# One wait for all casts of a group, in place of a wait per quarter, ahead of TensorE's transposes

## The chip, the cores and the metric

The kernel runs on one core of a Trainium2 chip. The metric is device microseconds of one execution, taken as the median of several.

## The reference

```python
def setup_inputs():
    b1, b2, m, k, n = 8, 16, 256, 512, 384
    return {"x": randn(b1, b2, m, k), "weight": randn(b1, b2, k, n)}   # float32 (cut)

def reference(x, weight):
    return np.matmul(x, weight).astype(np.float32)
```

These are 128 independent products of 256x512 by 512x384.

## The kernel before

Four products make a group, and there are 32 groups. SyncE issues all transfers: for each group two loads of w, one of x, and one store. ScalarE casts x to bfloat16 in four quarters (q). TensorE transposes each quarter (two bfloat16 values packed in a float32 word), VectorE copies the transposed quarter out of PSUM, TensorE multiplies, ScalarE copies the product to `out_sb`. VectorE also casts w.

```python
    XS, WS, OS = 2, 2 * G // D, 4       # buffers of x (groups), w (halves), out (groups)
    BS, TS, WBS = 1, 2, 2 * G           # of cast x, transposed x, cast w
    PT, PO = 4, 2                       # PSUM tiles: transposes, products
    LAG = 4                             # loads run four groups ahead of the stores
    ...
    def load(e, t, U, s):               # SyncE: two w loads, then the x load
        ...
                e.wait_ge(w_cast, n * (G * S) + ((d + 1) * D * S - 2 * G * S))
        ...
            e.wait_ge(x_cast, n * T + (1 - XS) * T)
    ...
    def multiply(e, t, U, s):           # TensorE
        n = t * U + s
        words = x_bf[s % BS][:].rearrange("p r s q c -> p r (s q c)").bitcast(fp32)
        for q in range(T):
            e.wait_ge(x_cast, n * T + (q + 1))
            e.wait_ge(t_copied, n * T + (q + 1 - PT + BIAS))
            for rr in range(2):
                for h in range(KO // 2):
                    ins = e.transpose(
                        pt[(s * T + q) % PT][:, rr, h, :],
                        words[:, 2 * q + rr, h :: KO // 2],
                        identity[:],
                    )
            ins.then_inc(t_made, 1)
        e.wait_ge(w_cast, n * (G * S) + G * S)
        for q in range(T):
            e.wait_ge(t_copied, n * T + (q + 1 + BIAS))
            e.wait_ge(o_copied, n * T + (q + 1 - PO + BIAS))
            for rr in range(2):
                for ko in range(KO):
                    for i in range(G):              # four products side by side
                        mine = slice(i * C, (i + 1) * C)
                        ins = e.matmul(po[...][mine, rr, :N], x_t[...], w_bf[...], ...)
            ins.then_inc(p_made, 1)
    ...
    def on_sync(e):
        ...
                load(e, t, U, LAG + s)
                store(e, t, U, s)
```

The order in the one transfer queue is thus w, w, x of group n+4, then the store of group n: a store always goes out behind an x.

## Time and profile before

| | before |
|---|---|
| median of 3 runs, us | 518.9 (518.43 to 518.95) |
| span of the profiled run, us | 517.2 |
| DMA queue, share of 16 engines' time | 99.3% |
| busiest compute engine (VectorE) | 64% |
| TensorE matmul / weight load | 59% / 39% |

The table is read from the bottom up: no compute engine is near the span, and the transfers fill it. The prediction below shows the lines. In the timeline, ScalarE's casts are followed in brackets by ScalarE's idle time before them and by what ended it. That idle time is the room between the chain of compute and the arrival of x:

```profile
114.30 3.89 ACT L132 CAST x_bf<-x_sb 128x1024 bf16<-128x1024 f32 x4 [3.76 <-DMA x_sb<-in_x_dram]
...
241.52 3.89 ACT L132 CAST x_bf<-x_sb 128x1024 bf16<-128x1024 f32 x4 [4.21 <-DMA x_sb<-in_x_dram]
```

### The profile page before, as it was taken

To read this page: it belongs to the slowest core of one execution; us is meant where nothing else is said; L and a number is where in the kernel's file an instruction comes from. 1 tells how busy PE (TensorE), PEld (TensorE's weight loads), DVE (VectorE), ACT (ScalarE), POOL (GpSimd) and SP (SyncE) were. 2 spreads that over 40 slices of the span, in tenths; PEclk is the share of its full clock that TensorE was granted. 3 is DMA by queue.
4 is the path that set the end of the run, shared out by engine and by line. 5 is a ranking of instruction groups with operands and counts; after the bars stand their busy time and mean duration, and the time that the engine had idled before them with its cause. 6 is when DMAs were issued, how large, how long until landed. Compare 5 with 4: busy or idle time off the path is not lost.

```text
span 517.2 us, 11523 instructions
## 1 busy us (share of the span) xinstructions
PE 306.6 (59%) x4608; PEld 200.6 (39%) x4608; DVE 332.8 (64%) x384; ACT 236.7 (46%) x264; POOL 0.7 (0%) x6
## 2 busy tenths in 40 slices
PE   0478776556665457645577554776446765467752
PEld 0345444334443334433344332444324443244431
DVE  3698875667556676556675566855658656676550
ACT  0465564443644436435355354454444544544441
POOL 0000000000000000000000000000000000000000
PEclk9998877878777887878777778877788877778777
DMA  8999999999999999999999999999999999999996
GB/s 340 430 423 424 424 432 426 429 428 430 432 427 427 427 428 432 429 427 430 426 431 431 426 429 430 427 432 427 427 429 429 427 433 425 430 428 430 429 428 251
DMA packets 18869, 218.18 MB, mean 422 GB/s; under 512 B 2096, under 2 KB 2096, under 8 KB 2608
## 3 DMA queue, kind: packets, MB, share of 16 engines
q1 hardware_dynamic: 18864, 218.11, 99.3%
q8 instruction: 3, 0.05, 0.0%
q14 instruction: 2, 0.02, 0.0%
HBM read 167.77 MB, written 50.33 MB: 422 GB/s over the span
## 4 chain that ended last, share of the span: by engine, by line
DMA 81%; ACT 10%; PE 4%; issue 3%; ACTq 0%; SPq 0%
DMA x_sb<-in_x_dram 81%; ACT x_bf L132 9%; PE po L180 2%; PE pt L166 1%; ACTq L130 0%; ACT out_sb L194 0%; SPq L111 0%; SPq L103 0%; ACT L132 0%; ACTq L193 0%; SPq L282 0%; SPq L55 0%
## 5 line engine op out<-in xcount | busy, mean ns | idle before, releaser
L147 DVE CAST w_bf<-w_sb 64x1536 bf16<-64x1536 f32 x256 | 244.4, 955 | 47.2 <-DMA w_sb<-in_weight_dram 38.5
L166 PE MATMUL pt<-identity,x_bf 128*128 128x128 f32 x512 | 123.7, 425 | 199.3 <-ACT x_bf L132 199.1
L180 PE MATMUL po<-w_bf,x_t 128*32 128x384 bf16 x4096 | 185.1, 342 | 1.0 <-issue 1.0
L166 PEld LDWEIGHTS pt<-identity,x_bf 128*128 128x128 f32 x512 | 91.8, 216 | 232.1 <-issue 218.3
L194 ACT COPY out_sb<-po 128x768 f32<-128x768 f32 x128 | 102.2, 798 | 147.2 <-PE po L180 147.2
L153 DVE COPY x_t<-pt 128x1024 bf16<-128x1024 bf16 x128 | 88.4, 691 | 122.3 <-PE pt L166 121.8
L132 ACT CAST x_bf<-x_sb 128x1024 bf16<-128x1024 f32 x128 | 124.4, 1042 | 80.9 <-DMA x_sb<-in_x_dram 80.8
L180 PEld LDWEIGHTS po<-w_bf,x_t 128*32 128x32 bf16 x4096 | 108.8, 101 | 73.8 <-issue 14.2
L132 ACT ACT_TABLE_LOAD x8 | 10.3, 1283 | 42.9 <-DMA x_sb<-in_x_dram 42.9
masks.py:199 POOL TENSOR_SCALAR_AFFINE_SELECT identity<-identity 128x128 f32<-128x128 f32 x1 | 0.3, 292 | 0.2 <-POOL identity L200 0.2
L200 POOL MEMSET identity<- 128x128 f32 x1 | 0.2, 204 | 0.5 <-SPq L55 0.5
L271 POOL MEMSET const-bfloat16-1.0<- 128x1 bf16 x1 | 0.1, 101 | 0.0
L271 POOL MEMSET const-uint8-127<- 128x1 uint8 x1 | 0.1, 101 | 0.0
L271 POOL MEMSET const-float32-0.0<- 128x1 f32 x1 | 0.1, 98 | 0.2 <-issue 0.2
L271 POOL MEMSET const-float32-1.0<- 128x1 f32 x1 | 0.1, 98 | 0.0
## 6 DMA issues: line engine op xcount, KB each, us to landing
w_sb<-in_weight_dram SPq DMA_DIRECT2D x64, 1536.0 KB, 27.5
x_sb<-in_x_dram SPq DMA_DIRECT2D x32, 2048.0 KB, 27.5
out_dram<-out_sb SPq DMA_DIRECT2D x31, 1536.0 KB, 30.7
out_dram<-out_sb SPq DMA_DIRECT2D x4, 384.0 KB, 5.9
```

The costliest lines, as they stand in the source:

```text
L132: e.copy(out=x_bf[s % BS][:, rows], in_=x_sb[s % XS][:, rows].rearrange("p r (q s c) -> p r s q c", s=S, c=KO),).then_inc(x_cast, 1)
L147: e.tensor_copy(out=w_bf[(s * G + d * D + a) % WBS][h * HP : (h + 1) * HP], in_=w_sb[slot][a * HP : (a + 1) * HP, h * KO : (h + 1) * KO, : ...
L153: e.tensor_copy(out=x_t[s % TS][:, 2 * q : 2 * q + 2], in_=pt[(s * T + q) % PT][:].bitcast(bf16),).then_inc(t_copied, 1)
L166: ins = e.transpose(pt[(s * T + q) % PT][:, rr, h, :], words[:, 2 * q + rr, h :: KO // 2], identity[:],)
L180: ins = e.matmul(po[(s * T + q) % PO][mine, rr, :N], x_t[s % TS][:, 2 * q + rr, ko // 2, mine, ko % 2], w_bf[(s * G + i) % WBS][:, ko, :], ...
L194: e.copy(out=out_sb[s % OS][:, 2 * q : 2 * q + 2, :], in_=po[(s * T + q) % PO][:, :, :N],).then_inc(o_copied, 1)
L200: e.memset(identity[:], 0.0).then_inc(id_done, 1)
L271: nc = _bacc.Bacc("TRN2", target_bir_lowering=False, num_devices=1)
```

## The change

TensorE waits until all four quarters of a group's x are cast, then does its 16 transposes in one run. The intent: TensorE rests while the casts run, which is when the store queued behind that x goes out.

```diff
         words = x_bf[s % BS][:].rearrange("p r s q c -> p r (s q c)").bitcast(fp32)
+
+        e.wait_ge(x_cast, n * T + T)
         for q in range(T):
-            e.wait_ge(x_cast, n * T + (q + 1))
             e.wait_ge(t_copied, n * T + (q + 1 - PT + BIAS))
```

## The prediction

> **What bounds the kernel now.** I read the page first: how busy the engines are against the DMA, and what share of the DMA queue's time is used.
>
> ```profile
> PE 306.6 (59%) x4608; PEld 200.6 (39%) x4608; DVE 332.8 (64%) x384; ACT 236.7 (46%) x264; POOL 0.7 (0%) x6
> ...
> DMA  8999999999999999999999999999999999999996
> ...
> q1 hardware_dynamic: 18864, 218.11, 99.3%
> ...
> HBM read 167.77 MB, written 50.33 MB: 422 GB/s over the span
> ...
> DMA 81%; ACT 10%; PE 4%; issue 3%; ACTq 0%; SPq 0%
> ```
>
> No compute engine is busy for more than 64% of the 517.2 us span, while the 16 DMA engines are busy for 99.3% of it and show a 9 in all slices but the first and last. The chain that ended last is 81% loading of x. Each group moves 2 x 1536 KB of w, 2048 KB of x and 1536 KB of out, 6.82 MB. Over 32 groups that is 218 MB, which at 429 GB/s takes 508 us. What is left is the start and the end. So the question for the change is not how long TensorE takes, but whether the DMA queue ever runs empty because of it.
>
> Next I asked for engine times in chosen stretches (columns: stretch, its length, busy us and count of PE, PEld, DVE, ACT, POOL, then TensorE clock, DMA share, GB/s).
>
> ```profile
> 4.00:16.00 12.00, 0.00 (x0) 0.00 (x0) 7.07 (x8) 0.00 (x0) 0.00 (x0) 1.00 1.01 431
> 100.00:300.00 200.00, 124.75 (x1860) 81.67 (x1862) 130.97 (x152) 93.26 (x105) 0.00 (x0) 0.78 1.01 429
> 498.00:501.00 3.00, 3.00 (x14) 2.34 (x15) 1.50 (x3) 2.55 (x3) 0.00 (x0) 0.50 1.01 430
> 502.00:506.00 4.00, 4.00 (x104) 2.71 (x100) 0.29 (x1) 1.97 (x3) 0.00 (x0) 1.00 1.00 424
> 514.00:516.00 2.00, 0.00 (x0) 0.00 (x0) 0.00 (x0) 0.00 (x0) 0.00 (x0) 0.50 0.04 17
> ```
>
> The reader is to see that the DMA moves 431 GB/s with TensorE wholly idle, 429 in the steady state, and 430 in a stretch where TensorE does nothing but transposes. The rate does not follow TensorE.
>
> Third, one group in the order of time, which gives the length of every step that the change touches.
>
> ```profile
> 258.69 3.89 ACT L132 CAST x_bf<-x_sb 128x1024 bf16<-128x1024 f32 x4
> 259.86 0.73 PEld L166 LDWEIGHTS pt<-identity,x_bf 128*128 128x128 f32 x4 [7.32 <-issue]
> 259.87 3.96 PE L166 MATMUL pt<-identity,x_bf 128*128 128x128 f32 x16 [6.94 <-ACT x_bf L132]
> 260.80 0.73 PEld L166 LDWEIGHTS pt<-identity,x_bf 128*128 128x128 f32 x4 [0.21 <-issue]
> ...
> 262.75 0.33 SPq L111 DMA_DIRECT2D x_sb<-in_x_dram  x1
> ...
> 273.31 3.89 ACT L132 CAST x_bf<-x_sb 128x1024 bf16<-128x1024 f32 x4 [2.41 <-DMA x_sb<-in_x_dram]
> ```
>
> Four casts take 3.89 us. TensorE follows them one by one: 0.73 us of transposes, a gap of about 0.22, the next four. The load of the x two groups later is issued 0.17 us after the last cast (258.69 + 3.89 = 262.58), and does not wait for TensorE.
>
> **What the Trainium skill says.** (1) "DMA: Bandwidth & Descriptors", Specifications, gives a fabric ceiling of 435 GB/s for a core's 16 DMA engines. The trace agrees: 429 to 431 GB/s, so at most 1.4% could be won from a better rate. (2) "SBUF — State Buffer", Who interferes with whom: DMA never contends with a compute engine. The trace agrees, 431 against 429 to 430 as shown. So letting TensorE rest while a store goes out has no transfer to speed up. (3) "TensorE: Matmul & The Clock Gate", Part 1: the clock is half until the engine has been busy for a window of 3413 ns. The trace shows a clock of 0.50 in 498 to 501 us, at the start of a run, and 1.00 in 502 to 506, so a shorter run of transposes may leave more matmuls at the half clock.
>
> **The change, part by part.** It removes three of four waits on the casts per group and makes the first wait for all four. It moves the 16 transposes; it adds and removes no work of an engine.
>
> (a) Start of the transposes: now after the first cast (1.04 us), then after the fourth (3.89), so 2.85 us later.
> (b) Their length: now the cast pace, 3 x 0.95 + 0.73 = 3.6 us. Then 4 x 0.73 = 2.9 us without gaps (an estimate from the 0.73; VectorE's copies of 0.69 us keep up with this, and the four PSUM buffers that they need were emptied in the group before).
> (c) So the matmuls start 2.85 + 2.9 - 3.6 = 2.1 us later. Clock: if the transposes' run is 0.7 us shorter, some 0.7 us more of the matmuls falls at half clock, which costs about 0.35 us on average. Sum: each group's copy to out_sb ends 2.1 to 2.6 us later, and so do VectorE's copies and the next w casts behind them.
>
> None of this is on the path that sets the end while the DMA queue has work. An x load takes a median of 27.5 us from issue to landing, of which its own 2.1 MB at 429 GB/s is 4.9 us. The other 22 us are other transfers ahead of it: that is the slack. A w load (27.5 us, 3.7 of its own) has 24 us. Against that, w loads come 2.1 to 2.6 us later and x loads not at all, unless ScalarE is late. Its idle time before the casts in the steady state is 2.41 to 4.79 us, so at worst a cast starts 0.2 us late.
>
> **The start** is tighter. There ScalarE is idle for under 1 us before the casts of groups 2 to 4 (0.28, 0.95, 0.24), so the delay adds up: about 2.2 us for each of the first five or six groups, some 8 to 10 us at most. Then it shrinks, because a group's chain on ScalarE (casts to last copy: 12 us now, 14.4 then, and 1.3 more in one of four) is still shorter than the 15.9 us that the DMA needs for a group. In those groups an x load lands 20 to 24 us after issue, so 15 to 19 us of slack, which covers it. Counting bytes issued against 429 GB/s, I find at least some 7 us of queued work at each issue (estimate).
>
> **The end** is where a delay could show in full. From the timeline, and the landing times of the stores issued at 492.9 us (group 30) and at 507.7 us (the last quarter of group 31):
>
> ```profile
> 501.49 5.38 PE L180 MATMUL po<-w_bf,x_t 128*32 128x384 bf16 x128
> ...
> 506.92 0.80 ACT L194 COPY out_sb<-po 128x768 f32<-128x768 f32 x1 [0.50 <-PE po L180]
> ```
>
> ```profile
> DMA to landing us min/median/max: 19.2/19.2/19.2
> ```
>
> ```profile
> DMA to landing us min/median/max: 8.0/8.0/8.0
> ```
>
> Group 30's store lands at 492.9 + 19.2 = 512.1. The four quarters behind it, 1.57 MB, take 3.7 us at 429 GB/s, and the last lands at 507.7 + 8.0 = 515.7, just 3.6 us after. So the slowest DMA engine was working off stores back to back up to the end (the others ran dry about 512: share 0.22, then 0.04), and the last piece sat in its queue. How late may that piece come? The first w load took 7.7 us from an empty queue, 3.7 of it transfer, so 4.0 us of latency; a quarter needs 4.0 + 0.9 = 4.9. Issued 2.1 to 2.6 us later, at 509.8 to 510.3, it would land at 514.7 to 515.2, still before 515.7. I expect 0 here, 0.5 us at the outside. **Sum**: 0 in the middle, 0 at the start, 0 to 0.5 at the end.
>
> **The rivals.**
> - The delay reaches the end: the engines that ran dry at 512 us show that the queue is nearly empty there. If the slowest engine is less slow in the next run, all 2.1 to 2.6 us show: 521.0 to 521.5, slower by 0.5%. Against it: 515.7 - 512.1 is the bare transfer time.
> - The store is helped by a resting TensorE, as the change intends. All stores are 50.3 MB, some 117 us at 429 GB/s. If these alone ran at 435, 1.6 us would be won, and at that rate throughout 7 us (512). Against it: 431 GB/s with TensorE idle, and the store is issued after the casts and lands 30.7 us later (page, section 6), so what goes out just then is older work anyway.
> - ScalarE or VectorE becomes the bound through the longer chain: about 14.4 us a group plus 1.3/4 is under 15.9, with 1 us to spare. If the matmuls fell to half clock altogether (LDWEIGHTS of four per 0.32 us instead of 0.16, so up to 10 us instead of 5.4), the chain would be 18 us and the kernel 8 to 13% slower. For it: TensorE idles longer before a run. Against it: the clock needs one busy window, and transposes plus matmuls are a run of over 8 us.
>
> **The range and the chances.** Now 518.9, with three runs from 518.43 to 518.95. My sum adds 0 to 0.5; I say 519.0. The low edge, 518.1, is a run as good as the best with a little of the second rival; the high edge, 520.4, is most of the first rival. 2% is 10 us: slower needs a bound that changes (the third rival, 1%), faster needs more than the whole gap to the fabric ceiling (1%). Within 2%: 98%.
>
> **What would show it right or wrong.** In the profile after: DMA still at 9 throughout and about 429 GB/s; TensorE's wait for the casts moved to one wait per group; 16 transposes in some 2.9 us; the matmuls some 2.1 us later after the casts' start (now 263.75 - 258.69 = 5.1, then about 7.2); ScalarE's idle time before the casts shorter by 2 us; x loads landing after nearly the same 27.5 us; the last store piece issued some 2 us later and landing in less than 8.0 us. I am wrong if slices in the middle show a DMA share below 9, if the x casts start later than x lands in the steady state, or if the rate differs from 429 by over 1%.

## The result

| | before | after |
|---|---|---|
| median of 6 runs, us | 518.64 (518.33 to 518.95) | 519.20 (518.98 to 519.51) |
| ratio, 95% interval | | 1.0011 (0.9998 to 1.0024) |
| span of the profiled run, us | 517.2 | 517.7 |

A ratio here is the mean time of one kernel's fast runs over that of the other's fast runs of the same rounds, so it is not quite the ratio of the medians. The two are the same within 2%. The difference of 0.56 us is small against the interval, but no run of after was as fast as the slowest of before, so I looked for it as well.

The page of after, the lines that answer to those of before:

```profile
PE 300.4 (58%) x4608; PEld 212.9 (41%) x4608; DVE 332.9 (64%) x384; ACT 235.9 (46%) x264; POOL 0.7 (0%) x6
...
DMA  8999999999999999999999999999999999999995
...
q1 hardware_dynamic: 18864, 218.11, 99.2%
...
DMA 56%; PE 22%; ACT 15%; issue 5%; ACTq 1%; SPq 0%
```

The DMA is as full as before. The chain that ended last, though, has lost a third of its x loads to TensorE and ScalarE: for part of the run, the chain of compute no longer waits for x. The time hardly moved, which is a warning that a chain's shares are not a cost.

One group of after in the steady state, from the timeline:

```profile
259.43 3.88 ACT L132 CAST x_bf<-x_sb 128x1024 bf16<-128x1024 f32 x4
263.44 3.29 PEld L167 LDWEIGHTS pt<-identity,x_bf 128*128 128x128 f32 x16 [8.17 <-issue]
263.45 3.68 PE L167 MATMUL pt<-identity,x_bf 128*128 128x128 f32 x16 [7.79 <-ACT x_bf L132]
263.49 0.33 SPq L111 DMA_DIRECT2D x_sb<-in_x_dram  x1
...
267.06 5.74 PE L181 MATMUL po<-w_bf,x_t 128*32 128x384 bf16 x128
...
274.08 3.88 ACT L132 CAST x_bf<-x_sb 128x1024 bf16<-128x1024 f32 x4 [0.42 <-DMA x_sb<-in_x_dram]
```

The matmuls of the matching group of before (its casts, at 258.69, stand in the prediction):

```profile
263.75 6.29 PE L180 MATMUL po<-w_bf,x_t 128*32 128x384 bf16 x128
```

The transposes are one run now, and the matmuls start 7.63 us after the casts' start (267.06 - 259.43), where before it was 5.06 (263.75 - 258.69): 2.57 us later. The load of the next x is still issued just after the last cast. ScalarE's room before the casts went from 2.41 to 0.42 us in the matching group.

In the first third of the run that room is gone altogether. These casts follow ScalarE's own earlier work without a wait, until the last line, the first with a wait for x since the first group:

```profile
106.19 3.88 ACT L132 CAST x_bf<-x_sb 128x1024 bf16<-128x1024 f32 x4
119.94 3.88 ACT L132 CAST x_bf<-x_sb 128x1024 bf16<-128x1024 f32 x4
...
178.51 3.88 ACT L132 CAST x_bf<-x_sb 128x1024 bf16<-128x1024 f32 x4 [0.46 <-DMA x_sb<-in_x_dram]
```

And the end. The last piece of the store is issued at 512.0 us in after (507.7 before) and lands in 4.3 us instead of 8.0, so at 516.3 instead of 515.7.

```profile
501.17 3.68 PE L167 MATMUL pt<-identity,x_bf 128*128 128x128 f32 x16 [6.54 <-ACT x_bf L132]
...
504.78 6.33 PE L181 MATMUL po<-w_bf,x_t 128*32 128x384 bf16 x128
...
511.17 0.80 ACT L195 COPY out_sb<-po 128x768 f32<-128x768 f32 x1 [0.50 <-PE po L181]
```

So the last group's compute ended 4.25 us later (511.17 against 506.92), and the program ended 0.5 us later.

### The profile page after: what moved, and what is told of

It reads as the page before. It is cut to its first block, busy times and chain, and to the rows that moved or that the text cites. A ratio compares the mean times of both kernels' runs of the same rounds, so it can differ in the third digit from the quotient of the medians.

```text
span 517.7 us, 11427 instructions
## 1 busy us (share of the span) xinstructions
PE 300.4 (58%) x4608; PEld 212.9 (41%) x4608; DVE 332.9 (64%) x384; ACT 235.9 (46%) x264; POOL 0.7 (0%) x6
## 3 DMA queue, kind: packets, MB, share of 16 engines
q1 hardware_dynamic: 18864, 218.11, 99.2%
## 4 chain that ended last, share of the span: by engine, by line
DMA 56%; PE 22%; ACT 15%; issue 5%; ACTq 1%; SPq 0%
DMA x_sb<-in_x_dram 56%; PE po L181 14%; ACT x_bf L132 14%; PE pt L167 8%; ACT L132 1%; ACTq L130 1%; ACT out_sb L195 0%; SPq L103 0%; SPq L111 0%; ACTq L194 0%; ACTq L246 0%; SPq L283 0%; SPq L55 0%
## 5 line engine op out<-in xcount | busy, mean ns | idle before, releaser
L167 PE MATMUL pt<-identity,x_bf 128*128 128x128 f32 x512 | 115.8, 418 | 210.8 <-ACT x_bf L132 210.8
L167 PEld LDWEIGHTS pt<-identity,x_bf 128*128 128x128 f32 x512 | 104.0, 225 | 222.6 <-issue 222.6
L181 PEld LDWEIGHTS po<-w_bf,x_t 128*32 128x32 bf16 x4096 | 109.0, 102 | 75.2 <-issue 16.1
## 6 DMA issues: line engine op xcount, KB each, us to landing
w_sb<-in_weight_dram SPq DMA_DIRECT2D x64, 1536.0 KB, 25.2
x_sb<-in_x_dram SPq DMA_DIRECT2D x32, 2048.0 KB, 26.4
```

The source lines that it names most:

```text
L167: ins = e.transpose(pt[(s * T + q) % PT][:, rr, h, :], words[:, 2 * q + rr, h :: KO // 2], identity[:],)
L181: ins = e.matmul(po[(s * T + q) % PO][mine, rr, :N], x_t[s % TS][:, 2 * q + rr, ko // 2, mine, ko % 2], w_bf[(s * G + i) % WBS][:, ko, :], ...
```

## The experiments

**Theory 1**: the transfers set the end; the queue hides the delay, and the end hides nearly all of it. **Rival, steady state**: the small loss comes from the groups in the middle, from a transfer rate that depends on what TensorE does. **Rival, any delay shows**. Twelve kernels ran, in three calls; each call had its own runs of before, on its own chip.

### Where is the 0.5 us?

First the changed kernel once more, as a yardstick.

> The changed kernel unaltered, as a yardstick beside the others of this call. Both theories: about 0.5 us above before (0.1%), as in the first result (519.2 against 518.64), if that difference is real; if it is run-to-run noise, anything from -0.3 to +0.6 us.

Measured: 519.06 us against 518.66 of before, ratio 1.0012 (0.9998 to 1.0026). So the 0.4 to 0.56 us came twice, though this time the fastest run of after (518.85) was not slower than the slowest of before (518.92).

Next, the new wait in all groups but the last (`late` is the changed wait):

```diff
-        with nc.Fori(0, NG // U, ...) as t:
+        with nc.Fori(0, NG // U - 1, ...) as t:
             for s in range(U):
-                multiply(e, t, U, s)
+                multiply(e, t, U, s, late=True)
+        multiply(e, 0, NG, NG - 2, late=True)
+        multiply(e, 0, NG, NG - 1, late=False)
```

> The late transposes in the first 31 groups, the old interleaving in the last one. Theory 1 (the queue hides the delay in the steady state, and what little shows comes from the end): as before, 518.6, within 0.2 us. Rival (the small loss comes from the steady state, from a transfer rate that depends on what TensorE does): about 519.2, as the changed kernel.

Measured: 519.39 us, ratio 1.0013 (0.9999 to 1.0026). And the reverse, with `late` true in the last group alone:

> The old interleaving in the first 31 groups, the late transposes in the last one alone. Theory 1: between 518.6 and 519.2; all of the small loss if the end carries it, with the last store piece issued some 2.5 to 4 us later than in before and landing in about 4 to 5 us instead of 8. Rival (steady state): 518.6, as before.

Measured: 518.68 us, ratio 1.0000 (0.9986 to 1.0014).

This went against theory 1 in its second half. The end costs nothing that shows: with the delay in the last group only, the last piece is issued at 510.3 us and lands 5.2 us later, at 515.5. With the last group early it is issued at 508.6 and lands 7.6 us later, at 516.2. The small loss goes with the first 31 groups. That rests on the medians and on the runs (all 519.16 or more, against 518.92 at most for before); the intervals of the ratios overlap.

### Does the transfer rate depend on TensorE?

All compute removed; a load waits for the landing of the load that had its buffer (out is zero):

```diff
-                e.wait_ge(w_cast, ...)            # and x_cast for x, o_copied for stores
+                e.wait_ge(w_in[slot], ...)        # and x_in for x; stores: the memsets alone
-    on_gpsimd; on_vector; on_tensor; on_scalar
+    for o in out_sb: nc.vector.memset(o[:], 0.0)
```

> The same loads and stores in the same order, with no cast, transpose, matmul or copy (out is zero: wrong on purpose). A load waits for the landing of the load that had its buffer, so two groups are in flight. It shows what the transfers alone cost when TensorE rests all the time. Theory 1: 516 to 519 us, i.e. at most 0.5% under before, at the same 429 GB/s in the middle. Rival (TensorE's work slows the stores, and rest helps them): 1 to 2% under before, 508 to 513 us, with a rate in the middle of 433 GB/s or more.

Measured: 517.32 us, ratio 0.9977 (0.9964 to 0.9991). The whole of the compute, with TensorE's work in it, costs this kernel 0.23%. That is the most that any rest of TensorE could win.

The opposite: before, with 16 dummy transposes after each group's matmuls.

```diff
             ins.then_inc(p_made, 1)
+        for _ in range(16):
+            e.transpose(pt[(s * T) % PT][:, 0, 0, :], identity[:], identity[:])
```

> The kernel before with 16 dummy transposes after each group's matmuls, in TensorE's idle time (the gap there is 4.4 us or more in the steady state; they take some 3.3 us), so that TensorE rests far less while stores go out. Theory 1: 518.6 as before, within 0.3 us, 429 GB/s in the middle. Rival (TensorE's activity slows the transfers): slower by 0.3% or more, and a lower rate.

Measured: 518.94 us against 518.86, ratio 1.0001 (0.9987 to 1.0015), TensorE busy 70% instead of 59%. Nothing. But these are transposes; matmuls beside a store are tested further down.

### How much delay is hidden?

The changed kernel with 4, 8 and 16 dummy transposes ahead of each group's first one:

```diff
+            if q == 0:
+                for _ in range(extra):            # 4, 8 or 16
+                    e.transpose(pt[(s * T) % PT][:, 0, 0, :], identity[:], identity[:])
```

> The changed kernel with 4 more transposes (of the identity, into a buffer that is overwritten) ahead of each group's 16, some 0.8 us more delay a group. In the fill of the changed kernel one group's chain on ScalarE takes 14.4 us on average; this makes 15.3, still under the DMA's 15.9. Theory 1: within 1 us of the changed kernel, 519 to 520.5. Rival (any delay shows): 519.2 + 32 x 0.8 = 545.

> 8 more transposes a group, some 1.65 us. The chain takes 16.1 us, just over the DMA's 15.9: theory 1 has the kernel bound by the chain now, 32 x 16.1 + 17.4 to the first x, less what the last group does not need, some 523 to 535 us, and the DMA share falling below 9 tenths or ScalarE no longer waiting for x. Rival (the transfers bound it whatever TensorE does): 519 to 520.

> 16 more transposes a group, some 3.3 us. Chain 17.7 us. Theory 1: 17.4 + 32 x 17.7 + about 5 = 585 to 595 us, slower by 13%, which shows where the slack ends. Rival (hidden whatever it is): 519 to 523.

| extra transposes a group | time, us | ratio to before | DMA rate |
|---|---|---|---|
| 0 (the change, first result) | 519.20 | 1.0011 | 429 (100 to 300 us) |
| 4 | 519.73 | 1.0018 | 429 (60 to 460 us) |
| 8 | 521.37 | 1.0049 | 429 (60 to 460 us) |
| 16 | 542.36 | 1.0466 | 421 (60 to 460 us) |

The rates come from the stretches of the two traces (columns as in the prediction), with 8 and with 16:

```profile
60.00:460.00 400.00, 262.00 (x3900) 204.16 (x3893) 264.50 (x308) 191.24 (x215) 0.00 (x0) 0.83 1.01 429
```

```profile
60.00:460.00 400.00, 273.11 (x3977) 219.72 (x3976) 253.40 (x300) 182.16 (x206) 0.00 (x0) 0.82 1.01 421
```

The slack does end, at the place where the chain of a group passes the 15.9 us that its transfers need. With 16 the chain took 16.2 us (four groups from 180.63 to 245.49), and 32 of these plus the 17.4 us to the first x is 536, with the last store still to come. I had expected 17.7 a group and 585 to 595 us; with 8 a group took 15.4 (217.54 to 278.98), not 16.1, and the 521.37 us lie between the two ranges (519 to 520 and 523 to 535), so both missed. The reason is in the timeline: the extra transposes bring TensorE to its full clock sooner, so that the 16 real ones run faster. With 16 extra ones:

```profile
204.31 2.08 PE L172 MATMUL pt<-identity,x_bf 128*128 128x128 f32 x16
206.32 5.38 PE L186 MATMUL po<-w_bf,x_t 128*32 128x384 bf16 x128
```

The clock is 1.00 from 204.3 us on here, and 0.50 in the run of transposes shown for after (263.4 to 267.06). The 16 real transposes take 2.08 us (up to 3.0 in other groups), where they took 3.68 after a rest, and the matmuls 5.38 where they took 5.74 or 6.33. So part of each added delay is paid back.

With 8 there is a riddle: the rate in the middle is full, yet 2.5 us were lost.

### One DMA engine of sixteen

A transfer is spread over 16 engines, each of which reports its share. I took the landing times of the shares from the traces: how far the slowest of the 16 is behind their median. With 8 extra transposes 15 engines stay on time (x of the last group lands at 493.8 in the median, and in before too), and the slowest share goes from 1.7 us behind at 200 us to 4.1 at 300. It loses 0.4 to 0.5 us at each store from 227 to 275 us, less at the two after those, and nothing at the loads. In these stores some packets of 12,288 bytes took 61 to 89 ns over the usual 460, one after the other. In each case TensorE was in its matmuls then (225.9 to 231.3 us, 241.4 to 247.0, and so on).

The same series of slow packets stands in the changed kernel, at 114.6 to 116.2, 129.5 to 132.1, 145.9 to 148.5 and 162.3 us, 1.2 us in sum. These are matmul stretches of the part where ScalarE has no room, so the store behind x falls beside the matmuls:

```profile
113.45 5.74 PE L181 MATMUL po<-w_bf,x_t 128*32 128x384 bf16 x128
...
127.28 5.65 PE L181 MATMUL po<-w_bf,x_t 128*32 128x384 bf16 x128
...
142.73 6.45 PE L181 MATMUL po<-w_bf,x_t 128*32 128x384 bf16 x128
```

Four of the four profiled kernels with the late wait in the loop and up to 4 extra transposes have such a series in the first 165 us; none of the three with the early wait (before, the one with only the last group late, the one with dummies after the matmuls) has more than two or three slow packets there; before has one only at its very end, from 502.7 to 506.4 us, beside the last group's matmuls. The slowest share shows the same split: by 200 us it was 2.5, 2.0, 2.5 and 2.4 us behind in the four, up 0.4 to 0.7 from the first load, and 1.8, 1.7 and 1.5 in the three, up 0.2 at most. So a new theory: **TensorE's matmuls slow the store on one DMA engine.** The last four runs test it on transfers alone, each with one engine's work running without pause.

The kernel's packed matmuls:

```diff
+    with nc.Fori(0, 85, ...):                     # 85 x one group's 128 matmuls
+        ...  nc.tensor.matmul(po[q % PO][mine, rr, :N], x_t[0][..., mine, ...], w_bf[0][:, ko, :], ...)
```

> Transfers only (out zero: wrong on purpose), with TensorE doing the kernel's packed matmuls (128x32 weights, 384 columns, four side by side) without pause for some 460 to 500 us on constant data. In the traces with more delay, one DMA engine's packets of a store took 61 to 99 ns over the usual 460 when the store fell beside this matmul phase. If TensorE's matmuls cause it: every store on that engine loses some 0.5 us, 27 x 0.5 = 13 us in all, so some 530 us against 517.3 of the transfers alone. If they do not: 517 to 518.5.

The same with all 128 columns in one instruction where those have four (`mine` becomes the whole 128):

> As the run before, with matmuls that use all 128 columns, so one instruction where that has four (some 6 a us instead of 24). If the cost follows TensorE's busy time or its reads: the same loss as the run before. If it follows the number of instructions (each leaves a record[...]): a fourth of it or nothing.

ScalarE's copies out of PSUM and VectorE's casts, both without pause:

> Transfers only, with ScalarE copying a PSUM tile to a spare one of 128x768 and VectorE casting 64x1536, the two other works of the matmul phase, without pause (ScalarE about 420 us or more, VectorE about 460). If one of these two causes the slow store packets: some 530 us. If TensorE does: 517 to 518.5.

Transposes of the identity:

> Transfers only, with TensorE doing transposes (of the identity) without pause for some 460 us: the change is to keep these away from the store. If they slow a store: above 518.5, at most some 530. If not: 517 to 518.5, and the rest that the change gives has nothing to win.

| transfers and ... | time, us | ratio to before | slowest share behind the median, us, at 7 / 100 / 200 / 300 / 450 us |
|---|---|---|---|
| nothing | 517.32 | 0.9977 | 0.5 / 0.4 / 1.8 / 1.8 / 1.7 |
| packed matmuls (to 464 us) | 528.20 | 1.0184 | 0.5 / 1.8 / 4.6 / 7.8 / 12.9 |
| whole matmuls (to 490 us) | 519.61 | 1.0020 | 0.7 / 2.0 / 2.1 / 2.0 / 3.3 |
| ScalarE and VectorE | 518.22 | 0.9992 | 0.5 / 0.2 / 1.3 / 2.2 / 2.0 |
| transposes (they ran to 249 us) | 518.88 | 1.0007 | 1.6 / 2.3 / 2.7 / 2.8 / 2.8 |

The packed matmuls cost 2.1% (1.0184 / 0.9977, on two chips; against before alone 1.67 to 2.01%, clear of zero). From 132 us on the slowest share lost 0.3 to 0.5 us at every store while TensorE worked, and nothing at the two stores after it stopped. The end of the two traces shows it without any sorting (stretches; VectorE and GpSimd columns as well, then clock, DMA share, GB/s). Transfers alone:

```profile
508.00:512.00 4.00, 0.00 (x0) 0.00 (x0) 1.00 0.95 383
512.00:516.00 4.00, 0.00 (x0) 0.00 (x0) 1.00 0.11 44
```

With packed matmuls:

```profile
512.00:516.00 4.00, 0.00 (x0) 0.00 (x0) 0.00 (x0) 0.00 (x0) 0.50 0.11 47
516.00:520.00 4.00, 0.00 (x0) 0.00 (x0) 0.00 (x0) 0.00 (x0) 0.50 0.06 28
520.00:524.00 4.00, 0.00 (x0) 0.00 (x0) 0.00 (x0) 0.00 (x0) 0.50 0.06 25
```

A share of 0.06 is one engine of 16 (0.0625), working on alone from about 516 us to the last landing at 525.4. The mean rate in the middle, 428 to 429 GB/s in both, does not show it.

ScalarE and VectorE are not the cause. The transposes show no loss at the stores. Their 518.88 is 0.3% above transfers alone, and much of that is 1.1 us by which one engine is behind from the very first load, before any store; there a packet of 16 KB of instructions, fetched at 6.0 us, took 0.93 us. The other traces fit this packet as the reason: beside the matmuls, packed and whole, the first one came at 23.6 and 23.5 us, and the slowest share went from 0.5 and 0.6 to 2.0 between the loads that landed at 23 and 28 us; in the two traces without one (transfers alone, ScalarE and VectorE) it stayed at 0.5 beyond 60 us. No run changes the packet by itself. Whole matmuls lose about 0.1 us a store, late in the run. Nor has every loss to do with compute: with transfers alone the slowest share went from 0.4 to 1.8 us between 100 and 200 us.

**What stays open.** The packed form has four times the instructions of the whole form in the same time (some 24 a microsecond against 6), but it also streams its 384 columns four times. Whether the reads or the instructions (each of which leaves a record in these profiled runs) slow that engine, no run here tells. Nor does any tell why it is one engine of the 16. And that the slow packets are the whole of the 0.5 us is argued, not shown: of the two profiles of the changed kernel one ended at 516.3 and one at 515.6 us, though both have the series. What does hold in the traces is that the end follows the slowest share. It was behind by 2.6 us at 450 us in before, 3.3 and 2.5 in these two, 5.1 with 8 extra and 12.9 with packed matmuls; the last landing was at 515.8, 516.3, 515.6, 518.3 and 525.4.

## Why the prediction was right, and where its steps were not

- **The bound**: right. DMA 99.2%, 429 GB/s in the middle; transfers alone take 517.3 us, so the kernel had 0.23% to give.
- **Start of the transposes 2.85 us later**: right; 4.02 us after the casts' start against 1.18.
- **Transposes 2.9 us in a run**: wrong. On the same measure, the weight loads, it is 3.29, 0.21 each; on TensorE 3.68 instead of 3.96. So one run saves 0.28 us and not 0.7. I divided a burst of four by four, but in a burst the second load starts 0.10 us after the first and the others follow at some 0.2.
- **Matmuls 2.1 us later, copies 2.1 to 2.6**: the matmuls' step was too small by just this term (2.84 - 0.28 = 2.56, and 2.57 was measured); in the steady group the last copy started 13.42 us after the casts' start instead of 11.41, 2.0 later, since the matmuls took 5.74 us and not 6.29. In the last group the matmuls were 2.79 later (7.62 against 4.83), and 0.96 more passed until the first copy, for the half clock at the start of the matmuls (507.27 - 504.78 = 2.49, before 503.02 - 501.49 = 1.53).
- **ScalarE's room, 2.41 to 4.79 us, less the delay**: right; 0.42 to 2.20 from group 11 on, and none in one group (cast at 337.82), where it was used up.
- **The start, a delay of 8 to 10 us that then shrinks**: right; the casts of group 5 came at 91.97 instead of 82.49 us, 9.5 later; a group's chain took 14.4 us there (33.79 to 119.94, six groups), and the gap closed by group 11 (178.51 against 177.92). The queue had enough: w loads took a median of 25.2 us to land, x loads 26.4, both 27.5 before.
- **The end, 0 to 0.5 us**: the step failed as put, though the number held. The last piece came 4.3 us later, not 2.1 to 2.6. In the run with only the last group late it came 2.6 us later and cost nothing (1.0000); the full 4.3 was not tested by itself, but with the end early again in all_but_last (508.6) nothing was won back. The 0.5 us that I allowed for the end came from the first 31 groups, so that my number is so near is luck. I had worked with 4.0 us of latency before a piece's own 0.9; in the last-only run one landed 3.6 us after issue in all.
- **The third rival, matmuls at half clock**: did not come; from 60 to 460 us a group's matmuls took 5.4 to 6.5 us in after, not 10.
- **"The rate does not follow TensorE"**, and with it the second rival: right for the mean, and wrong as a statement on all engines. One engine of 16 slows down beside packed matmuls, and the mean of 16 hides it. It was also beside the point that the store issued after the casts goes out 30 us later: the queue always holds an older store right behind x, and it is this one that the change means to protect. The change does not win, because in the steady state of before, x lands (for the slowest engine at 241.4 us) and its store takes until about 245, while the matmuls begin at 246.6: the store was beside transposes, which cost it next to nothing. The delay puts some stores of the start beside the matmuls instead.

## What to carry to other kernels

When one transfer queue is full from start to end, ask of a change to compute only how much it eats of the room: how long ago the loads were issued, and how far the chain of a group is under the time its transfers need. Then test the edge by adding delay in doses; here 4 extra transposes cost no more than the change itself within the noise (1.0018 against 1.0011), and 16 cost 4.7%. A mean over 16 engines can be perfect while one of them falls behind, and a transfer lands when the last share does: look at the tail of the run, where a share of 1/16 is one engine alone.

## What the Trainium skill lacked or had wrong

- "SBUF — State Buffer", Who interferes with whom, has DMA never contend with a compute engine. Transfers alone took 517.3 us, and 528.2 with packed matmuls beside them, nearly all of the loss on one DMA engine's stores. ScalarE and VectorE at work without pause: 518.2. Whether the reads or the instruction records do it is open; if it is the records, the page is not contradicted.
- "TensorE: Matmul & The Clock Gate", Part 4, has the full clock not engage for transposes. Here transposes alone held it at 1.00 from 20 to 240 us, and it fell to 0.50 after they ended; in before it rose from 0.50 (498 to 501 us) through 0.83 to 1.00 at 501.5, with nothing but transposes done since the rest. Sixteen of them took 3.68 us after a rest and 2.08 at the full clock (float32 words; the page's times are of bfloat16).
- "DMA: Bandwidth & Descriptors" calls two of the 16 engines usually slower, but has no figure for how far one may fall behind the others' median (which engine it is, these traces do not tell): 1.6 us from the first load on in before, 2.8 at 485 us, 12.9 at 450 us with packed matmuls.
